# A two-layer hybrid backbone in f32 on one core: latent operands formed in place, early feed-forward products, chained transfers of the down projection

## The chip, the core and the metric

The kernel runs on one core of a Trainium2 chip. TensorE (PE) multiplies, VectorE (DVE) and GpSimd (POOL) work elementwise, ScalarE (ACT) applies functions of one operand, SyncE (SP) issues the DMAs. SBUF holds the operands, PSUM the products. The metric is the device time of one execution in microseconds; less is better.

## The reference

Two layers over 1024 latent and 256 context tokens of width 1024, all in f32. Layer 0 mixes by a convolution and a bidirectional state-space model, layer 1 by grouped-query attention, in which the context gives only keys and values. Each layer ends as follows (the context only in layer 0):

```python
x = layer_norm(ALPHA * x + g_m * y_lat, ln_g[l, 0], ln_b[l, 0])
x = layer_norm(ALPHA * x + g_f * swiglu(modulate(x, sh_f, sc_f), w_ffn_in[l], w_ffn_out[l]),
               ln_g[l, 1], ln_b[l, 1])
def swiglu(h, w_in, w_out):
    gate, up = jnp.split(h @ w_in, 2, axis=-1)
    return (jax.nn.silu(gate) * up) @ w_out
```

`y_lat` is the mixer's output behind its output projection; `g_m`, `sc_f`, `sh_f`, `g_f` are vectors made from the conditioning. The hidden width is 2816, 22 tiles of 128.

## The kernel before

Tokens lie along the free dimension, features along the partitions. The blocks `BLK` are 0 and 1 (512 latent tokens each) and 2 (256 context tokens, layer 0 only); a block's activations are eight tiles of 128 features, `acc(nb, k)`. Every f32 operand of a large product is split into two parts, a rounded `high` (L275, ScalarE) and the remainder `low` (L278, VectorE or GpSimd), and `mm3` (L293) makes three matmuls per product of tiles: high by high, high by low, low by high.

`out_proj` (L1597) runs blocks 0, 1 and, in layer 0, 2; for each of eight output tiles it loads and splits a weight (`weights`, L282 with L275 and L278), multiplies 24 times, loads the residual, scales it on GpSimd (L1626), adds the product on VectorE (L1627) and adds the tile to the running row sum on GpSimd (`add_up`, L411). Behind each block it starts `norm` (L444): a matmul with ones spreads the mean (L401), VectorE centres each tile (L449), ScalarE squares it (L452), VectorE adds the squares (L455), matmuls with a column of ones give the variance (L420), ScalarE takes the root (L423), VectorE the reciprocal (L424), matmuls broadcast the factor r over the partitions (L428), and ScalarE copies it to SBUF (L462). Then block 0 goes to `first_operands`, block 1 to `second_operands`, the context to `apply`. These multiply by r (L521, L531), form `a z + b` with gain a and bias b of the modulated norm on ScalarE (L541, L487) and VectorE (L543, L489), and split the result. The normalised tiles are stored to `res` by `put` for the residual of the down projection.

`ffn` handles gate and up, of both latent blocks, for one hidden tile f by seven products of 12 matmuls instead of eight (a Strassen-Winograd scheme). With A11, A12 the two feature halves of block 0 and A22 the second half of block 1, S1 to S4 are sums and differences of the halves of both blocks; on the weights' side B11, B12, B21, B22 and T1 to T4, made by `quads` (GpSimd's subtractions at L585, splits L275 and L278). The order in a tile is:

```python
p = multiply("A11", "B11")
p = multiply("A12", "B21")
late = multiply("S4", "B22")
seventh = multiply("S3", "T3")
p = multiply("S2", "T2")
p = multiply("S1", "T1")
p = multiply("A22", "T4")
```

In layer 0 the context's gate and up products (48 matmuls of 256 columns) follow in each tile; in tile 0 they stand behind S1 and need the context's norm. The hidden tiles, in two parts, go to DRAM (`hide`, L675).

The down projection (`run`) walks blocks 0, 2, 1 (layer 1: 0, 1), four output tiles at a time (`lower`, `upper`), over pairs j of hidden tiles. `last_weights` loads and splits the weights of a pair, `load` (L757) brings hidden tiles back from DRAM into 28 free slots, `residual` fetches `res` (L509) and scales it on GpSimd (L765 to L771).

Within a phase TensorE's order is pinned by `in_order`. VectorE, ScalarE, GpSimd and SyncE get their order from a scheduler that walks the program by estimated due times; each engine then works strictly in that order. `PACE` tables tell the scheduler how long a background task, such as a norm, takes between its steps. `fixed`, `hurry`, `loose` and `urgent` loosen or raise single instructions.

## Time and profile before

| | |
|---|---|
| Median of 3 runs | 2898.48 us (2891.24 to 2900.97) |
| Profiled execution | 2894.89 us, span from first to last instruction 2892.9 us |
| Mean granted clock of TensorE | 0.957 of full speed |
| Busy: TensorE, VectorE, GpSimd, ScalarE | 91%, 65%, 39%, 39% |
| DMA | 395.12 MB, mean 137 GB/s |
| TensorE waiting in `mm3` for an operand's high part | 50.0 us in 8 waits |
| TensorE waiting in `mm3` for a weight's high part | 27.2 us in 8 waits |

Names of tiles in the trace: `p` is a product in PSUM, `n` a mean, variance or r in PSUM, `hl`, `x`, `xr` hold operands, `wsplit` weights in two parts, `raw` weights as loaded, `acc` activations, `tmp` scratch, `hid` hidden tiles in DRAM, `res` stored activations in DRAM. A timeline row gives start, length, engine, line, operation, tiles written and read, the count of instructions run together and, in brackets, the engine's idle time before and what ended it. Some small f32 matmuls leave two records each.

### The profile page before, as it was taken

Reading aid. Unit: us, or ns where it says so; the run is one execution under the profiler, and the core shown is the slowest. Engines: PE = TensorE matmul, PEld = TensorE weight load, DVE = VectorE, ACT = ScalarE, POOL = GpSimd, SP = SyncE. Lnnn points to the kernel's source line nnn. Section 1 sums busy time; section 2 is a strip of 40 time slices with the busy share of each in tenths; the row PEclk is TensorE's granted clock in tenths of the full one; section 3 lists DMA queues with packets and bytes.
Section 4 is the critical chain, followed back from the end, with each engine's and each line's share of the span. In section 5 each row is a group of like instructions: output and inputs, shape, how many; then the busy total and the mean of one; then the engine's idle time right before and its main releaser. Section 6 shows DMA issues by size and latency. Waiting matters only on the chain.

```text
span 2892.9 us, 38248 instructions
## 1 busy us (share of the span) xinstructions
PE 2642.9 (91%) x14324; PEld 2223.6 (77%) x14324; DVE 1889.3 (65%) x2844; ACT 1119.3 (39%) x1943; POOL 1127.4 (39%) x994
## 2 busy tenths in 40 slices
PE   7867899949999999899999999999957999998998
PEld 4756777738888888788887778898846888886887
DVE  8876647887777655324458569998578666652244
ACT  5211216443333333123334348888344333331133
POOL 2799543444333433101035225554445444421111
PEclk9978999969999999999999999999978999999998
DMA  7322556314444222966444421112422323247634
GB/s 268 89 57 56 161 187 249 115 65 158 167 161 144 111 99 99 352 203 222 132 135 127 121 66 52 52 59 73 153 80 88 114 105 117 108 151 294 217 126 131
DMA packets 184233, 395.12 MB, mean 137 GB/s; under 512 B 38000, under 2 KB 74352, under 8 KB 177264
## 3 DMA queue, kind: packets, MB, share of 16 engines
q1 hardware_dynamic: 184048, 392.68, 40.3%
q8 instruction: 113, 1.85, 0.3%
q14 instruction: 72, 0.59, 0.1%
HBM read 305.11 MB, written 82.28 MB: 134 GB/s over the span
## 4 chain that ended last, share of the span: by engine, by line
PE 70%; DVE 10%; POOL 8%; DMA 7%; issue 2%; ACT 1%; SPq 1%; DVEq 0%; POOLq 0%; ACTq 0%
PE p L293 59%; PE q L293 3%; PE p L1874 3%; DMA raw<-w_ffn_out 2%; PE p L1857 2%; DVE const L1834 2%; DVE wsplit L278 1%; DVE tmp L531 1%; POOL acc L1020 1%; POOL acc L1023 1%; DVE const L1824 1%; DVE hl L278 1%; DMA hl<-hid 1%; DMA acc<-res 1%; PE p L1365 1%
## 5 line engine op out<-in xcount | busy, mean ns | idle before, releaser
L293 PE MATMUL p<-hl,wsplit 128*128 128x512 f32 (+1 forms) x5604 | 1201.2, 372 | 102.7 <-ACT hl L275 50.0
L293 PEld LDWEIGHTS p<-hl,wsplit 128*128 128x128 f32 x5604 | 973.9, 192 | 313.2 <-ACT hl L275 56.7
L278 DVE TENSOR_TENSOR wsplit<-raw,wsplit 128x1024 fp32r<-128x1024 f32 (+1 forms) x307 | 352.3, 1149 | 422.7 <-ACT wsplit L275 402.5
L275 ACT ACTIVATE wsplit<-raw 128x1024 fp32r<-128x1024 f32 (+1 forms) x368 | 316.0, 863 | 775.7 <-PE p L293 456.0
L293 PE MATMUL p<-x,wsplit 128*128 128x512 f32 (+1 forms) x1408 | 333.8, 384 | 1.3 <-DVE hl L1368 0.8
L293 PEld LDWEIGHTS p<-x,wsplit 128*128 128x128 f32 x1408 | 258.8, 190 | 53.4 <-ACT x L275 1.0
L667 DVE TENSOR_TENSOR tmp<-p,tmp 128x512 f32<-128x512 f32 x308 | 206.1, 684 | 67.9 <-PE p L293 59.2
L293 PE MATMUL p<-hl,acc 128*128 128x512 f32 x996 | 232.8, 389 | 0.0
L278 POOL TENSOR_TENSOR wsplit<-raw,wsplit 128x512 fp32r<-128x512 f32 (+1 forms) x61 | 101.8, 1672 | 315.3 <-ACT wsplit L275 308.9
L585 POOL TENSOR_TENSOR raw<-raw 128x512 f32<-128x512 f32 (+1 forms) x99 | 184.7, 1866 | 96.1 <-DVE wsplit L278 50.3
L293 PEld LDWEIGHTS p<-hl,acc 128*128 128x128 f32 x996 | 186.4, 188 | 38.3
L411 POOL TENSOR_TENSOR tmp<-tmp,acc 128x512 f32<-128x512 f32 (+1 forms) x54 | 85.6, 1586 | 251.6 <-DVE acc L810 184.3
L1874 PE MATMUL p<-hl,acc 128*128 128x256 f32 x960 | 150.8, 294 | 12.2 <-DVE hl L278 8.9
L1874 PEld LDWEIGHTS p<-hl,acc 128*128 128x128 f32 x960 | 130.3, 191 | 24.8 <-DVE hl L278 15.5
L278 POOL TENSOR_TENSOR hl<-tmp,hl 128x512 fp32r<-128x512 f32 (+1 forms) x56 | 84.4, 1524 | 111.5 <-ACT hl L275 46.7
L293 PE MATMUL q<-hl,wsplit 128*128 128x512 f32 (+1 forms) x576 | 125.2, 378 | 0.0
L1916 POOL TENSOR_TENSOR tmp<-tmp 128x1024 f32<-128x1024 f32 x32 | 77.1, 2410 | 118.9 <-DMA tmp<-w_mod_rows 80.5
L293 PEld LDWEIGHTS q<-hl,wsplit 128*128 128x128 f32 x576 | 102.0, 206 | 19.1 <-issue 3.9
L278 DVE TENSOR_TENSOR hl<-p,hl 128x512 fp32r<-128x512 f32 x160 | 106.4, 681 | 8.8 <-ACT hl L275 7.1
L275 ACT ACTIVATE hl<-p 128x512 fp32r<-128x512 f32 x160 | 95.5, 598 | 31.0 <-PE p L1857 29.5
L293 PE MATMUL q<-acc,raw 128*128 128x512 f32 x384 | 104.3, 407 | 0.3 <-ACT hl L1840 0.3
L585 POOL TENSOR_TENSOR acc<-acc 128x512 f32<-128x512 f32 (+1 forms) x33 | 62.1, 1882 | 97.6 <-DVE wsplit L278 56.7
(403 smaller groups left out, 4018.7 us busy)
## 6 DMA issues: line engine op xcount, KB each, us to landing
raw<-w_ffn_out SPq DMA_DIRECT2D x121, 512.0 KB, 3.7
raw<-w_ffn_in SPq DMA_DIRECT2D x33, 1024.0 KB, 4.9
hid<-acc SPq DMA_DIRECT2D x66, 512.0 KB, 2.6
hl<-hid SPq DMA_DIRECT2D x60, 512.0 KB, 7.2
acc<-w_mod_rows SPq DMA_DIRECT2D x32, 512.0 KB, 3.6
tmp<-w_mod_rows SPq DMA_DIRECT2D x32, 512.0 KB, 3.5
x<-w_mod SPq DMA_DIRECT2D x28, 512.0 KB, 8.5
raw<-w_out_ab SPq DMA_DIRECT2D x24, 512.0 KB, 3.7
```

The lines of the kernel that those rows point to most:

```text
L275: self.nc.scalar.activation(dst.bitcast(F32R), src, AF.Copy, scale=scale)
L278: (eng or self.nc.vector).tensor_tensor(dst.bitcast(F32R), src, high, op=ALU.subtract)
L293: self.nc.tensor.matmul(ps, a.bitcast(F32R), b.bitcast(F32R), start=start and i == 0, stop=stop and i == 2)
L411: eng.tensor_tensor(self.sums, self.total, x, op=ALU.add)
L531: tt = lambda out, x, y, op: nc.vector.tensor_tensor(out, x, y, op=op)
L585: nc.gpsimd.tensor_tensor(out, x, y, op=ALU.subtract)
L667: tt = lambda out, a, b: nc.vector.tensor_tensor(out, a, b, op=ALU.add)
L1020: v.tensor_tensor(t, ai, bi, op=ALU.mult)
L1834: v.scalar_tensor_tensor(m[:, 1:2], m[:, 0:1], work[i]["c"][:, u:u + 1], rq, op0=ALU.min, op1=ALU.mult)
L1857: nc.tensor.transpose(pt[:, o:o + 128], p, bd.pk("ident"))
L1874: nc.tensor.matmul(po, val.bitcast(F32R), part[:, j * 256:(j + 1) * 256].bitcast(F32R), start=kp == 0 and e == 0, stop=kp == 4 and e == 5)
L1916: nc.gpsimd.tensor_tensor(w, w, c_row, op=ALU.mult)
```

## The change

Four parts.

**Latent blocks.** `latents` takes the place of `norm` with `first_operands` or `second_operands`. It stores the centred tiles, not the normalised ones, to `res` while centring, and the factor r to a tensor `factor` of its own. The gain is multiplied in place together with r, read from PSUM; the differences that make S4, S2, S3 are taken of tiles without a bias, and the biases, which follow from C_BS and the gains, enter in the split (`parts`). All low parts are on VectorE. For block 1 the squares are summed by TensorE: 32 matmuls with a column of ones, four after each tile. Sums and differences overwrite the tiles of both blocks in place; `mixing` holds back S2 and what follows until the early products have been written down.

**Output projection.** Row sums go to VectorE, residual scaling to ScalarE, two tiles at a time. The last block takes the output tiles in the order 7, 6, 5, 4, 0 to 3 and uses the split weights of 4 to 7 that the block before left in `KEPT`.

**Feed-forward.** The products A11·B11 and A12·B21 of the first `AHEAD` tiles (1 in layer 0, 3 in layer 1) stand ahead of block 1's operands; S2 comes before S3; the splits of T2, T3 and T1 of tile 0 come early; the context's norm begins behind S3 of tile 0. In layer 1 GpSimd makes the low part of T4 instead of B21.

**Down projection.** Weights are fetched in a list of needs, three pairs ahead, and `queue` ties each weight, hidden-tile and residual transfer to the one before it in program order. Six hidden tiles are begun in the last feed-forward tile. `residual` loads the factor, multiplies it in on VectorE and scales on ScalarE.

```diff
+    def queue(self):
+        if self.queued is not None:
+            self.after(self.latest(), self.queued)
+        self.queued = self.latest()
...
+    def parts(self, dst, x, bias=None):
+        h, lo = dst
+        if bias is None:
+            self.high(h, x)
+            self.low(lo, x, h)
+        else:
+            self.nc.scalar.activation(h.bitcast(F32R), x, AF.Identity, bias=bias)
+            self.nc.vector.scalar_tensor_tensor(lo.bitcast(F32R), x, bias, h, op0=ALU.add, op1=ALU.subtract)
...
+    def latents(self, nb, i, total, res):
...
+        self.stat(mean, total)
...
+        def add_squares():
+            k, s = todo.pop(0)
+            for j in range(n // 128):
+                nc.tensor.matmul(pv[:, j:j + 1], s[:, j * 128:(j + 1) * 128], ones,
+                                 start=k == 0 and j == 0, stop=k == KT - 1 and j == n // 128 - 1)
+                self.loose()
...
+        for k in range(KT):
+            tt(z[k], z[k], mean, ALU.subtract)
+            s = self.g(squares.next(), n) if last else self.t(n) if k else sq
+            nc.scalar.activation(s, z[k], AF.Square)
+            if k % 2:
+                nc.sync.dma_start(res[k - 1:k + 1, :, off:off + n].rearrange("k p n -> p k n"),
+                                  self.g3(ACC + ACO[nb], KT, n)[:, k - 1:k + 1])
...
+        factor = self.g(squares.next(), n) if last else sq
+        nc.scalar.activation(factor, r, AF.Copy)
+        nc.sync.dma_start(self.factors[nb], factor)
+        gain = lambda k: nc.vector.scalar_tensor_tensor(z[k], z[k], self.gains(i, nb, k)[0], r, op0=ALU.mult, op1=ALU.mult)
+        bias = lambda k: self.gains(i, nb, k)[1]
+        if not last:
+            for k in range(KT):
+                gain(k)
+                self.parts(self.operand("A11" if k < 4 else "A12", k % 4), z[k], bias(k))
+                yield pace[4]
+            for k in range(4):
+                tt(z[k + 4], z[k], z[k + 4], ALU.add)
+            return
+        y = [self.acc(0, k) for k in range(KT)]
+        for k in range(4):
+            gain(k)
+            gain(k + 4)
+            tt(z[k], z[k], z[k + 4], ALU.add)
+            tt(y[k + 4], y[k + 4], z[k], ALU.subtract)
+            self.parts(self.operand("S4", k), y[k + 4])
+        while self.mixing:
+            yield 1.0
+        for k in range(4):
+            tt(y[k], z[k], y[k], ALU.subtract)
+            self.parts(self.operand("S2", k), y[k], bias(k + 4))
+        for k in range(4):
+            tt(y[k + 4], z[k + 4], y[k], ALU.subtract)
+            self.parts(self.operand("S3", k), y[k + 4])
+        for k in range(4):
+            self.parts(self.operand("S1", k), z[k], self.g(C_BS + k, 1))
+        for k in range(4):
+            self.parts(self.operand("A22", k), z[k + 4], bias(k + 4))
...
+        begun = [following[0]] + [early(f) for f in range(1, ahead)]
+        for f in range(ahead):
+            p = self.ps()
+            self.product(p, "A11", begun[f]["B11"])
+            nc.scalar.activation(gates[f][:, 512:], p, AF.Copy)
+            p = self.ps()
+            self.product(p, "A12", begun[f]["B21"])
+            tt(gates[f][:, :512], p, gates[f][:, 512:])
+        self.mixing = False
...
-        def last_weights(ds, j):
-            if (ds, j) not in ready:
-                ready[ds, j] = self.weights(ow[j:j + 2, :, ds[0] * 128:(ds[-1] + 1) * 128].rearrange("f p n -> p f n"))
-            return ready[ds, j]
+        def last_weights():
+            if wanted:
+                ds, j = wanted.pop(0)
+                ready.append(self.weights(ow[j:j + 2, :, ds[0] * 128:(ds[-1] + 1) * 128].rearrange("f p n -> p f n"), queue=True))
...
         def residual(nb):
+            if nb < 2:
+                r = self.g(self.sum_ring.next(), 512)
+                nc.sync.dma_start(r, self.factors[nb])
+                self.queue()
             for d in range(0, KT, 2):
                 self.fetch(res, nb, d)
+                self.queue()
                 for k in (d, d + 1):
...
-                    nc.gpsimd.tensor_scalar(a, a, self.g(o + 32 + k, 1), self.g(o + 40 + k, 1), op0=ALU.mult, op1=ALU.add)
+                    if nb < 2:
+                        nc.vector.tensor_tensor(a, a, r, op=ALU.mult)
+                    nc.scalar.activation(a, a, AF.Identity, scale=self.g(o + 32 + k, 1), bias=self.g(o + 40 + k, 1))
```

Three places show how the instructions move; the line numbers of the changed kernel differ (`mm3` is L308, `low` L291, an eviction L1771, `add_up` L429, the squares L565, the gain L604, a low part with a bias L542).

TensorE in layer 1, from the end of the output projection; `p_...` are products, `n_...` means, variances and r. Before:

```order
L293 MATMUL p_16192<-hl_141_3271,wsplit_68 128x512 x12
L293 MATMUL p_16206<-hl_141_3271,wsplit_68 128x512 x12
L401 MATMUL n_16059<-tmp_69,const_60 128x512
L420 MATMUL n_16084<-const_60,tmp_69 128x1 x4
L428 MATMUL n_16091<-const_60 128x128 x4
L293 MATMUL p_16221<-hl_142_3272,wsplit_68 128x512 x12
```

With the change:

```order
L308 MATMUL p_16080<-hl_141_3271,wsplit_68 128x512 x12
L308 MATMUL p_16094<-hl_141_3271,wsplit_68 128x512 x3
L419 MATMUL n_16098<-tmp_69,const_60 128x512
L308 MATMUL p_16094<-hl_141_3271,wsplit_68 128x512 x9
L308 MATMUL p_16116<-hl_141_3271,hl_509_15460 128x512 x3
L565 MATMUL n_16100<-const_60,tmp_69 128x1 x4
L308 MATMUL p_16116<-hl_141_3271,hl_509_15460 128x512 x6
L565 MATMUL n_16100<-const_60,tmp_69 128x1 x4
L308 MATMUL p_16116<-hl_141_3271,hl_509_15460 128x512 x3
L308 MATMUL p_16143<-hl_141_3271,hl_509_15460 128x512 x3
L565 MATMUL n_16100<-const_60,tmp_69 128x1 x4
```

A mean, a variance and a broadcast stood in a row behind two products; now the mean stands inside the second product, and the squares of single tiles stand between further products with the same `hl_141_3271` (A11, A12) and other weights.

VectorE in layer 1, from block 0's factor to block 1's centring (`acc_504...` is block 0, `acc_505...` block 1, `hl_141...` A11 and A12). Before:

```order
L521 TENSOR_TENSOR acc_504_15441<-acc_504_15441,tmp_69 128x512 x8
L489 TENSOR_SCALAR tmp_69<-acc_504_15441,const_60 128x512 x3
L1627 SCALAR_TENSOR_TENSOR acc_505_15442<-p_15907,const_60,acc_505_15442 128x512
L489 TENSOR_SCALAR tmp_69<-acc_504_15441,const_60 128x512 x2
L278 TENSOR_TENSOR wsplit_68<-raw_15420,wsplit_68 128x512
L489 TENSOR_SCALAR tmp_69<-acc_504_15441,const_60 128x512
L1627 SCALAR_TENSOR_TENSOR acc_505_15442<-p_15954,const_60,acc_505_15442 128x512
L489 TENSOR_SCALAR tmp_69<-acc_504_15441,const_60 128x512 x2
L1627 SCALAR_TENSOR_TENSOR acc_505_15442<-p_15999,const_60,acc_505_15442 128x512
L278 TENSOR_TENSOR wsplit_68<-raw_15420,wsplit_68 128x512 x3
L449 TENSOR_TENSOR acc_505_15442<-acc_505_15442,n_16059 128x512 x8
```

With the change (the eight gains, L604, stand just ahead):

```order
L542 SCALAR_TENSOR_TENSOR hl_141_3271<-acc_504_15455,const_60,hl_141_3271 128x512 x4
L429 TENSOR_TENSOR tmp_69<-tmp_69,acc_505_15456 128x512
L542 SCALAR_TENSOR_TENSOR hl_141_3271<-acc_504_15455,const_60,hl_141_3271 128x512
L1771 SCALAR_TENSOR_TENSOR acc_505_15456<-p_15957,const_60,acc_505_15456 128x512
L542 SCALAR_TENSOR_TENSOR hl_141_3271<-acc_504_15455,const_60,hl_141_3271 128x512 x3
L551 TENSOR_TENSOR acc_504_15455<-acc_504_15455 128x512
L1771 SCALAR_TENSOR_TENSOR acc_505_15456<-p_15999,const_60,acc_505_15456 128x512
L429 TENSOR_TENSOR tmp_69<-tmp_69,acc_505_15456 128x512
L551 TENSOR_TENSOR acc_504_15455<-acc_504_15455 128x512 x3
L291 TENSOR_TENSOR wsplit_68<-raw_15434,wsplit_68 128x512
L429 TENSOR_TENSOR tmp_69<-tmp_69,acc_505_15456 128x512
L551 TENSOR_TENSOR acc_505_15456<-acc_505_15456,n_16098 128x512 x8
```

The eight values with gain and bias (L489), whose low parts GpSimd made, have given way to eight low parts on VectorE (L542), pair sums of block 0 (L551) and row sums (L429).

SyncE in layer 1, around the start of the down projection. Before:

```order
L509 DMA acc_691_18978<-res_92 128x2x512
L757 DMA hl_142_3272<-hid_0_16027 128x1024
L757 DMA hl_142_3272<-hid_20_16047 128x1024
L282 DMA raw_15420<-w_ffn_out 128x2x512
L757 DMA hl_142_3272<-hid_1_16028 128x1024
L757 DMA hl_509_15446<-hid_4_16031 128x1024
L757 DMA hl_509_15446<-hid_2_16029 128x1024
L757 DMA hl_509_15446<-hid_5_16032 128x1024
L757 DMA hl_509_15446<-hid_3_16030 128x1024
L282 DMA raw_15420<-w_ffn_out 128x2x512
L675 DMA hid_21_16048<-acc_534_16182 128x1024 x2
L282 DMA raw_15420<-w_ffn_out 128x2x512
```

With the change:

```order
L295 DMA raw_15434<-w_ffn_out 128x2x512 x2
L807 DMA hl_141_3271<-hid_6_16036 128x1024
L807 DMA hl_141_3271<-hid_7_16037 128x1024
L295 DMA raw_15434<-w_ffn_out 128x2x512
L807 DMA hl_142_3272<-hid_8_16038 128x1024
L807 DMA hl_142_3272<-hid_9_16039 128x1024
L295 DMA raw_15434<-w_ffn_out 128x2x512
L807 DMA hl_142_3272<-hid_10_16040 128x1024
L807 DMA hl_142_3272<-hid_11_16041 128x1024
L784 DMA hid_21_16051<-acc_538_16292 128x1024 x2
L295 DMA raw_15434<-w_ffn_out 128x2x512
L807 DMA x_15458<-hid_12_16042 128x1024
```

Before, hidden tiles stood ahead of the weights of the second and third pairs; now a weight pair stands behind every second hidden tile, and the stores of the last hidden tile (`hid_21...`) stand ahead of the fifth pair.

## Rows read from the trace of the kernel before

**Rows 1.** The page: busy time of the engines, chain that ended last.

```profile
PE 2642.9 (91%) x14324; PEld 2223.6 (77%) x14324; DVE 1889.3 (65%) x2844; ACT 1119.3 (39%) x1943; POOL 1127.4 (39%) x994
...
PE 70%; DVE 10%; POOL 8%; DMA 7%; issue 2%; ACT 1%; SPq 1%; DVEq 0%; POOLq 0%; ACTq 0%
```

**Rows 2.** Stretches: length, engines' busy time (instructions), granted clock, DMA share, GB/s.

```profile
2240.00:2280.00 40.00, 40.00 (x178) 33.11 (x178) 27.08 (x36) 14.77 (x26) 17.58 (x11) 1.00 0.28 106
2040.00:2080.00 40.00, 40.00 (x178) 33.14 (x177) 13.98 (x14) 7.44 (x7) 21.63 (x15) 1.00 0.39 125
2149.40:2154.10 4.70, 3.92 (x16) 3.56 (x16) 0.61 (x2) 0.32 (x2) 0.00 (x0) 0.50 0.00 0
1203.38:1233.49 30.11, 21.90 (x72) 16.53 (x73) 6.12 (x5) 5.29 (x5) 8.31 (x10) 0.83 0.88 336
2619.64:2650.73 31.09, 18.96 (x72) 14.55 (x73) 4.90 (x4) 4.24 (x4) 6.82 (x8) 0.78 0.98 371
```

**Rows 3.** TensorE's timeline, layer 1: start, length, line, operation, count, [idle before].

```profile
2101.39 0.95 PE L420 MATMUL n<-const,tmp 128*128 128x1 f32 x8
...
2107.10 1.05 PE L428 MATMUL n<-const 128*128 128x128 f32 x8
2107.91 16.37 PE L293 MATMUL p<-hl,wsplit 128*128 128x512 f32 x71
...
2136.76 2.08 PE L401 MATMUL n<-tmp,const 128*128 128x512 f32 x2 [1.25 <-POOL tmp L411]
2149.52 1.84 PE L420 MATMUL n<-const,tmp 128*128 128x1 f32 x8 [10.69 <-DVE tmp L455]
2151.93 2.08 PE L428 MATMUL n<-const 128*128 128x128 f32 x8 [0.57 <-DVE const L424]
...
2200.60 5.60 PE L293 MATMUL p<-hl,acc 128*128 128x512 f32 x24
```

**Rows 4.** Waits of TensorE, 2060 to 2210: total, times, longest.

```profile
PE p L293 <- ACT hl L275: 25.4, 4, 10.0
```

**Rows 5.** VectorE's timeline, layer 1.

```profile
2089.26 1.21 DVE L278 TENSOR_TENSOR wsplit<-raw,wsplit 128x1024 fp32r<-128x1024 f32 x1
...
2105.72 2.36 DVE L278 TENSOR_TENSOR wsplit<-raw,wsplit 128x1024 fp32r<-128x1024 f32 x1 [0.16 <-ACT wsplit L275]
...
2124.89 0.74 DVE L1627 SCALAR_TENSOR_TENSOR acc<-p,const,acc 128x512 f32<-128x512 f32 x1
...
2154.67 4.90 DVE L531 TENSOR_TENSOR acc<-acc,tmp 128x512 f32<-128x512 f32 x8 [2.80 <-ACT tmp L462]
...
2165.24 0.68 DVE L278 TENSOR_TENSOR hl<-tmp,hl 128x512 fp32r<-128x512 f32 x1
```

**Rows 6.** TensorE's timeline, layer 0.

```profile
537.09 17.22 PE L293 MATMUL p<-hl,wsplit 128*128 128x512 f32 x87
...
559.18 3.13 PE L293 MATMUL p<-hl,wsplit 128*128 128x256 f32 x24 [0.53 <-DVE wsplit L278]
...
592.02 6.78 PE L293 MATMUL p<-hl,wsplit 128*128 128x512 f32 x24
...
654.88 7.79 PE L293 MATMUL p<-acc,wsplit 128*128 128x256 f32 x48 [9.06 <-ACT tmp L703]
```

**Rows 7.** VectorE's timeline, the context's norm in layer 0.

```profile
598.86 2.72 DVE L449 TENSOR_TENSOR acc<-acc,n 128x256 f32<-128x256 f32 x8
...
648.51 5.11 DVE L489 TENSOR_SCALAR tmp<-acc,const 128x256 f32<-128x256 f32 x8
```

**Rows 8.** TensorE's timeline, start of layer 1's down projection.

```profile
2631.21 8.40 PE L293 MATMUL p<-hl,wsplit 128*128 128x512 f32 x26 [11.57 <-ACT wsplit L275]
```

**Rows 9.** SyncE's timeline there (DMA issues).

```profile
2584.05 0.38 SPq L282 DMA_DIRECT2D raw<-w_ffn_out  x1
...
2619.69 0.38 SPq L282 DMA_DIRECT2D raw<-w_ffn_out  x1
```

**Rows 10.** TensorE's timeline, start of layer 0's down projection.

```profile
1208.70 9.04 PE L293 MATMUL p<-hl,wsplit 128*128 128x512 f32 x24 [5.32 <-ACT wsplit L275]
```

More of the change, by code (lines that the diff above doesn't have):

```diff
@@ L564, in quads @@
+    def quads(self, layer, f, direct, first=True):
         nc = self.nc
@@ L576, in split @@
             self.hurry()
-        split("B11", b11)
-        split("B21", b21)
+        if first:
+            split("B11", b11)
+            split("B21", b21)
         split("B22", b22)
@@ L732, in ffn @@
             if f == FT - 1:
-                last_weights(lower, 4)
+                last_weights()
             tt(gate2, p, gate2)
@@ L737, in ffn @@
             if f == 0:
-                following = self.quads(layer, 1, context)
+                following = self.quads(layer, 1, context, 1 >= ahead)
+            gate = gates[0]
         if after:
@@ L1610, in out_proj @@
             bd.finish(before[nb])
-        for d in range(KT):
-            if nb == blocks[1] and d == 1:
+        order = (7, 6, 5, 4, 0, 1, 2, 3) if nb == blocks[-1] else range(KT)
+        for step, d in enumerate(order):
+            if mods and nb == blocks[1] and step == 1:
                 bd.finish(*mods)
```

237 lines of the change are left out of this document (143 added, 94 removed).

## Prediction

> **What bounds the kernel now.** The shares of the page come first: TensorE is busy 91% of the span, VectorE 65%, and the chain that ended last is 70% TensorE, 10% VectorE, 8% GpSimd and 7% DMA [rows 1]. So time can only be won where TensorE stands still or runs slowly. The table of stretches says where that is not: in a feed-forward stretch TensorE is busy 40.00 of 40 us, 178 matmuls, 0.2247 us each [rows 2]. A product of 12 matmuls takes 2.7 us there, a group of 24 takes 5.4 us. VectorE (27.08), ScalarE (14.77) and GpSimd (17.58) have room.
>
> TensorE's timeline shows where it stands. In layer 1 the output projection's last group and tile 0's first product end at 2124.3 (2107.91 + 16.37), and tile 0's last product ends at 2203.3 (2200.60 and half of the 24 that follow) [rows 3]: 79 us for a tile whose remaining work is 16.2 us. The table of waits puts 25.4 us of it on four gaps before S4's operands [rows 4]; another 10.69 stands ahead of the variance [rows 3]. Layer 0 has the same gap between 592 and 655 [rows 6]. The third place is the start of the down projections: in layer 1 TensorE waits 11.57 us for a weight split [rows 8], and wait and 72 matmuls together take 31.09 us (2619.64 to 2650.73) instead of 16.2 [rows 2]: a loss of 14.9. SyncE had issued one weight load at 2584.05 and the next only at 2619.69, behind 28 other transfers [rows 9]. In layer 0 the wait is 5.32 [rows 10], and 72 matmuls from its start on take 30.11 [rows 2]: a loss of 13.9.
>
> **Layer 1, from the projection to tile 0.** In the change out_proj leads to latents, which forms the operands in place; its order on VectorE sets the new time, so I add it up with the durations of rows 5: 0.61 us for a two-tensor operation in a run (4.90 for 8), 0.68 alone, 0.74 for the eviction with a PSUM operand, which I also take for the gain (it reads r in PSUM). The bias form (a low part with a bias) is not in this trace: bounds 0.61 and 0.74, I take 0.68, since it reads SBUF alone.
> Block 0's r is broadcast 9 matmuls later in its group than before, so at 2108.2 + 2.0 = 2110.2 [rows 3]. VectorE then has, up to the last row sum, 8 gains (5.9), 3 evictions (2.2), 8 low parts (5.4), 4 pair sums (2.4), 3 row sums (1.8), one weight part (0.7): 18.4 us, to 2128.6. Before, the mean started at 2136.76, behind GpSimd [rows 3].
> From the mean to the last square TensorE's pinned order holds 54 product matmuls (12.1 us) and 32 squares; four squares are eight records of 0.95 us [rows 3], so 7.6 us. With 1.0 for the mean: 2149.3. Square root, reciprocal and broadcast took from 2151.36 (2149.52 + 1.84) to 2154.01 (2151.93 + 2.08) [rows 3]; 2.6 us give 2151.9. This chain is no shorter than the old one, but four products of tiles 1 and 2 lie in it (10.8 us that the tiles no longer need).
> After r VectorE has 8 gains (5.9), 12 two-tensor operations (7.3), 8 bias lows (5.4), 8 lows of S4 and S2 (5.2), 4 differences and 4 lows of S3 (5.2): 29.0, to 2180.9. Behind S3's last low come 3 matmuls, then S1 and A22: 6.1 us, to 2187.0, against 2203.3. The stretch wins 16.3 + 10.8 = 27.1.
> The clock takes some back. After TensorE had stood 10.69 us the eight variance records took 1.84 us against 0.95 elsewhere, the broadcast 2.08 against 1.05 [rows 3]: the granted clock was 0.50 there [rows 2], 1.2 instead of 2.4 GHz. The changed order leaves one wait of some 4 us before the mean. Layer 0's 24 product matmuls after waits took 6.78 instead of 5.4 [rows 6]; I take such a 1.4 once, with bounds 0 and 19.7 (everything from mean to r at half clock, the whole of 12.1 + 7.6 again). **Sum: 25.7, taken as 25 us**; bounds 8 (the clock's 19.7) and 33 (r as early as centring alone would let it be, 7 us of squares less).
>
> **Layer 0.** The context block follows block 1 and starts at 554.3 (537.09 + 17.22) [rows 6]. Its 8 groups at 3.13 [rows 6], the squares (7.6) and 1.5 for mean and broadcast make 34.2, to 588.5; the squares cost TensorE time here, where the old block had waits for weight splits (0.53 ahead of a group [rows 6]). r stands 37 small matmuls (4.8) before the end: 583.7. VectorE: 8 gains (5.9), the operand work as above with 3.0 of evictions and sums (15.7), S4 and S2 lows (5.2), S3 (5.2), early weight parts and evictions (2.7): to 618.4. The context norm now follows S3: centring 8 of 0.34 (2.72) [rows 7], squares' sums and three evictions 7, root and broadcast 4, scaling 2.7 and forming 5.1 [rows 7], the last low 1: to 641. The context's gate products start there, at 654.88 before [rows 6]; what stands behind them is the same. **14 us**; 5 if the context's norm waits for tile 0's other products as now (9 us), 22 if its centring finds VectorE free between S4's and S3's lows (8).
>
> **Down projections.** Weights and hidden tiles are now issued in the order of need, three weight pairs ahead: 1.5 MB for every step of 5.4 us, 280 GB/s, under the 371 GB/s that the old start moved [rows 2]. The stores of the last hidden tile still stand in SyncE's queue, ahead of the fifth weight pair; they wait for the last tile's VectorE work, some microseconds behind its last product, and that pair is needed 21 us later. The factor loads (0.25 MB a block) and the four residual loads are spread in between. **28 us of the 28.8 go**, 14 if only one of the two starts is mended.
>
> **What costs nothing.** Residual scaling goes from GpSimd to ScalarE: in layer 1, 16 operations at between 0.57 (14.77 / 26) and 1.06 us (7.44 / 7) each, 9 to 17 us, beside one weight split every 5.4 us on an engine busy 7.44 of 40 [rows 2]; if the residual's DMA came late the splits behind it in ScalarE's queue would wait, some 5 us. Row sums on VectorE: 8 of 0.61 per block beside the dense projection, VectorE busy 13.98 of 40 in block 0. The factor's 8 multiplications a block lie beside dense down products. Four fewer weight splits in the last block: only in cover, except in layer 0's context block, counted above.
>
> **Sum.** 25 + 14 + 28 = 67 us off the profiled execution of 2894.89 gives 2828; that execution lies 3.6 us (0.12%) under the median of the runs, so I predict 2830. The bounds give 27 (8 + 5 + 14) to 83 (33 + 22 + 28): 2812 to 2871 around the median. A measurement of this kernel can tell some 0.3%, 8.7 us.
>
> **Rivals.**
> *The queue is not mended.* The chained transfers stand behind one another: if the stores of hidden tile 21 or the residual loads hold SyncE, the wait for weights moves a few steps on instead of going. For it: the queue is in order, and a wait at its head stops the weights too. Against: three pairs are ahead. Time: 2830 + 28 = 2858; chance 0.13.
> *Half of the transitions.* ScalarE forms the eight high parts of A22 and S1 ahead of S4's and sits behind squares, copies and table loads; if it, not VectorE, sets each low, the 25 + 14 shrink to the early products' 10.8: 2830 + 28.2 = 2858 as well; chance 0.13.
> *VectorE slowed by GpSimd: slower than before.* In this trace one VectorE low of 128x1024 took 2.36 us at 2105.72, where GpSimd added, and 1.21 at 2089.26 [rows 5]. The changed transitions put some 47 us of VectorE work in layer 1 and 45 in layer 0 on the path. At double price throughout they would cost 92 more: 2830 + 92 = 2922. It decides from a mean price 73% higher (67 of 92) on. Against it: the order shows GpSimd almost empty there, its lows and sums gone. Chance 0.06.
> The Trainium skill ("SBUF — State Buffer", section "SBUF: two separate sides") says that a VectorE operation with two SBUF inputs and a GpSimd operation that reads SBUF exclude each other for a whole instruction; the 2.36 against 1.21 agrees, and by that rule an emptied GpSimd keeps VectorE at the lower price.
> *It changes nothing measurable.* The early products only change places with the tiles' own, and both partial cases together leave 10.8 of the 67; a mean in layer 1 halfway back to the old one (4 of 8 us [rows 3]) leaves 7, under what can be told: 2892; chance 0.05.
> The Trainium skill ("TensorE: Matmul & The Clock Gate", section "What's actually happening") calls the throttled clock the default that activity releases; by that rule the early products would keep the higher clock through the statistics and give back the 1.4 us, 2829.
>
> **How the numbers follow.** Forecast 0.63, the two partial cases 0.13 each, slower 0.06, no change 0.05. The likeliest is 2830. Leaving out the last two (0.11) and the tails of the others, the range runs from 2806 (all bounds good, and 6 us for the relief of engines that I priced at nothing) to 2872. Faster by over 0.3%: 0.63 + 0.26 = 0.89; within: 0.05; slower: 0.06.
>
> **What would show it.** Right: in layer 1 the mean 5 us behind the end of tile 0's first product instead of 12; A22 of tile 0 some 16 us earlier, and tiles 1 and 2 a product pair shorter; in layer 0 the context's gate some 14 us earlier, measured from the end of block 1's projection; no wait above 2 us at either down start, and a weight load every third transfer on SyncE. Wrong: a new wait in the tiles, where GpSimd now has T4's low part instead of B21's in layer 1; VectorE's lows at 1.2 us in the transitions; or granted clock still near 0.6 in them.

## The result and the profile after

The changed kernel takes 2824.36 us (median of 4 runs, 2822.47 to 2826.97), the kernel before 2894.86 beside it: a ratio of 0.9756, 95% interval 0.9732 to 0.978, or 70.5 us less. The forecast was 2830, faster. The profiled execution has a span of 2824.8 us, where the one of before has 2892.9 (68.1 less).

The page of the changed kernel, shares and chain [rows 1]:

```profile
PE 2644.6 (94%) x14436; PEld 2234.9 (79%) x14436; DVE 1859.5 (66%) x2899; ACT 1158.4 (41%) x2003; POOL 935.1 (33%) x839
...
PE 76%; DVE 9%; POOL 8%; DMA 4%; ACT 1%; issue 1%; SPq 1%; DVEq 0%; POOLq 0%; ACTq 0%
```

TensorE is busy for almost as long as before, in a span 68 us shorter, and DMA has fallen from 7% of the chain to 4. The next table cuts both traces at the same places of the program; each number is a difference of two starts on TensorE's timeline.

| stretch | before | after | change | forecast |
|---|---|---|---|---|
| layer 0: end of block 1's projection to the first product behind the context's gate | 108.2 | 96.1 | −12.1 | −14 |
| layer 0: the first 144 matmuls of the down projection | 46.6 | 32.6 | −14.0 | −13.9 |
| layer 1: start of tile 0's first product to its last operand A22 used | 81.7 | 65.8 | −15.9 | −16.3, clock +1.4 |
| layer 1: tiles 1 to 21 | 399.9 | 389.0 | −10.9 | −10.8 |
| layer 1: the first 144 matmuls of the down projection | 47.6 | 32.6 | −14.9 | −14.9 |
| all else | 2208.9 | 2208.7 | −0.2 | 0 |

TensorE's timeline of the changed kernel in layer 1 answers to [rows 3]:

```profile
2093.64 3.56 PE L308 MATMUL p<-hl,wsplit 128*128 128x512 f32 x15
2100.24 1.61 PE L419 MATMUL n<-tmp,const 128*128 128x512 f32 x2 [3.04 <-DVE tmp L429]
2100.87 4.15 PE L308 MATMUL p<-hl,wsplit 128*128 128x512 f32 x9
...
2105.54 0.95 PE L565 MATMUL n<-const,tmp 128*128 128x1 f32 x8
...
2123.07 1.09 PE L595 MATMUL n<-const 128*128 128x128 f32 x8
2136.28 0.79 PE L308 MATMUL p<-hl,wsplit 128*128 128x512 f32 x1 [12.11 <-ACT hl L288]
2143.73 4.97 PE L308 MATMUL p<-hl,wsplit 128*128 128x512 f32 x11 [6.66 <-DVE hl L291]
...
2156.74 5.60 PE L308 MATMUL p<-hl,acc 128*128 128x512 f32 x24
```

Read it from the top: the projection ends at 2093.64, the mean waits 3.04 us for VectorE's last row sum (before, it waited for GpSimd), then products and squares fill TensorE until r (L595) at 2123.07. Behind r it stands for 12.11 and 6.66 us, while VectorE makes the operands; then all the rest of the tile follows without a gap. VectorE's timeline shows the list that it stands behind (before: [rows 5]):

```profile
2125.20 5.35 DVE L604 SCALAR_TENSOR_TENSOR acc<-acc,const,n 128x512 f32<-128x512 f32 x8 [1.24 <-ACT tmp L602]
...
2139.27 1.28 DVE L551 TENSOR_TENSOR acc<-acc,acc 128x512 f32<-128x512 f32 x2
2140.47 0.74 DVE L542 SCALAR_TENSOR_TENSOR hl<-acc,const,hl 128x512 fp32r<-128x512 f32 x1
...
2151.67 1.28 DVE L291 TENSOR_TENSOR xr<-acc,x 128x512 fp32r<-128x512 f32 x2
```

The eight gains (L604) come first, S3's last low parts end at 2152.95, and no other work stands between. The first gain starts 1.04 us behind the end of r's broadcast; the wait is put down to ScalarE's copy of r (L602), which stands behind an activation and a table load. In layer 0 the same chain lies beside the context block (before: [rows 6]):

```profile
567.31 2.74 PE L565 MATMUL n<-const,tmp 128*128 128x1 f32 x24
...
571.06 4.70 PE L565 MATMUL n<-const,tmp 128*128 128x1 f32 x24
576.83 3.41 PE L565 MATMUL n<-const,tmp 128*128 128x1 f32 x16
...
584.73 1.27 PE L595 MATMUL n<-const 128*128 128x128 f32 x8
...
634.19 0.58 PE L308 MATMUL p<-acc,wsplit 128*128 128x256 f32 x1 [1.15 <-ACT acc L505]
637.10 5.19 PE L308 MATMUL p<-acc,wsplit 128*128 128x256 f32 x18 [2.33 <-POOL acc L291]
...
648.16 5.63 PE L308 MATMUL p<-hl,acc 128*128 128x512 f32 x24
```

The 64 squares take 10.85 us here, not the 7.6 of full clock, and the context's gate (48 matmuls, 634.19 to 648.16) takes 14.0 us where it took 7.6: it starts 18.5 us earlier, counted from the projection's end, and 6.3 of these are lost in it again, at a granted clock of 0.56. VectorE's last operand of S3 and GpSimd's first low part of the context there:

```profile
617.72 0.67 DVE L291 TENSOR_TENSOR xr<-acc,x 128x512 fp32r<-128x512 f32 x1
```
```profile
636.28 1.46 POOL L291 TENSOR_TENSOR acc<-tmp,acc 128x256 fp32r<-128x256 f32 x2 [49.09 <-DVE tmp L507]
```

The starts of the two down projections of the changed kernel, as stretches (those of before: [rows 2]); they have no wait at all:

```profile
1166.69:1204.77 38.08, 38.08 (x170) 31.53 (x168) 18.76 (x24) 15.06 (x18) 0.00 (x0) 1.00 0.99 356
2548.40:2581.06 32.66, 32.66 (x145) 27.03 (x144) 15.40 (x19) 11.51 (x15) 0.00 (x0) 1.00 0.96 352
```

And SyncE's timeline ahead of layer 1's, where [rows 9] had one weight load and then none for 35 us:

```profile
2564.06 0.38 SPq L295 DMA_DIRECT2D raw<-w_ffn_out  x1
...
2565.49 0.43 SPq L890 DMA_DIRECT2D tmp<-factor  x1
2566.66 4.34 SPq L527 DMA_DIRECT2D acc<-res  x4
2572.00 0.37 SPq L295 DMA_DIRECT2D raw<-w_ffn_out  x1
```

### The profile page after: what moved, and what is told of

Its sections match the earlier page's. It is cut to its first block, busy times and chain, and to the rows that moved or that the text cites. A ratio compares the mean times of both kernels' runs of the same rounds, so it can differ in the third digit from the quotient of the medians.

```text
span 2824.8 us, 38374 instructions
## 1 busy us (share of the span) xinstructions
PE 2644.6 (94%) x14436; PEld 2234.9 (79%) x14436; DVE 1859.5 (66%) x2899; ACT 1158.4 (41%) x2003; POOL 935.1 (33%) x839
## 4 chain that ended last, share of the span: by engine, by line
PE 76%; DVE 9%; POOL 8%; DMA 4%; ACT 1%; issue 1%; SPq 1%; DVEq 0%; POOLq 0%; ACTq 0%
PE p L308 64%; PE q L308 3%; PE p L2017 3%; PE p L2000 2%; DVE const L1977 2%; PE p L1494 1%; POOL acc L1149 1%; POOL acc L1152 1%; DMA raw<-w_ffn_out 1%; DVE const L1967 1%; PE p L350 1%; DVE wsplit L291 1%; DVE acc L551 1%; DVE hl L291 1%; POOL tmp L1150 1%
## 5 line engine op out<-in xcount | busy, mean ns | idle before, releaser
L308 PE MATMUL p<-hl,wsplit 128*128 128x512 f32 (+1 forms) x5004 | 1066.4, 371 | 49.2 <-DVE hl L291 18.5
L308 PEld LDWEIGHTS p<-hl,wsplit 128*128 128x128 f32 x5004 | 871.1, 191 | 234.2 <-DVE hl L291 25.3
L288 ACT ACTIVATE wsplit<-raw 128x1024 fp32r<-128x1024 f32 (+1 forms) x340 | 289.4, 853 | 655.1 <-PE p L308 328.8
L291 DVE TENSOR_TENSOR wsplit<-raw,wsplit 128x1024 fp32r<-128x1024 f32 (+1 forms) x280 | 305.1, 1091 | 379.6 <-ACT wsplit L288 366.0
L308 PE MATMUL p<-x,wsplit 128*128 128x512 f32 (+1 forms) x1422 | 328.7, 380 | 0.8 <-DVE hl L1497 0.8
L308 PEld LDWEIGHTS p<-x,wsplit 128*128 128x128 f32 x1422 | 256.7, 188 | 51.4 <-ACT x L288 1.0
L291 POOL TENSOR_TENSOR wsplit<-raw,wsplit 128x512 fp32r<-128x512 f32 (+1 forms) x60 | 99.8, 1668 | 510.6 <-ACT wsplit L288 504.7
L308 PE MATMUL p<-hl,acc 128*128 128x512 f32 x972 | 226.3, 389 | 0.0
L308 PEld LDWEIGHTS p<-hl,acc 128*128 128x128 f32 x972 | 182.3, 188 | 37.9 <-DVE acc L291 0.2
L661 POOL TENSOR_TENSOR raw<-raw 128x512 f32<-128x512 f32 (+1 forms) x99 | 182.2, 1840 | 83.4 <-DMA raw<-w_ffn_in 56.1
L308 PE MATMUL q<-hl,wsplit 128*128 128x512 f32 (+1 forms) x576 | 124.8, 377 | 0.0
L308 PEld LDWEIGHTS q<-hl,wsplit 128*128 128x128 f32 x576 | 101.3, 204 | 19.4 <-issue 3.9
L308 PE MATMUL p<-hl,x 128*128 128x512 f32 (+1 forms) x528 | 114.1, 363 | 0.0
L291 DVE TENSOR_TENSOR hl<-p,hl 128x512 fp32r<-128x512 f32 x160 | 106.4, 681 | 8.4 <-ACT hl L288 6.8
L288 ACT ACTIVATE hl<-p 128x512 fp32r<-128x512 f32 x160 | 95.5, 598 | 32.0 <-PE p L2000 30.6
L308 PE MATMUL q<-acc,raw 128*128 128x512 f32 x384 | 104.2, 406 | 0.3 <-ACT hl L1983 0.3
L308 PEld LDWEIGHTS p<-hl,x 128*128 128x128 f32 x528 | 91.1, 196 | 14.6 <-issue 1.0
L308 PE MATMUL p<-acc,wsplit 128*128 128x256 f32 x696 | 92.5, 291 | 3.9 <-POOL acc L291 2.7
```

Source lines behind the costliest of these rows:

```text
L288: self.nc.scalar.activation(dst.bitcast(F32R), src, AF.Copy, scale=scale)
L291: (eng or self.nc.vector).tensor_tensor(dst.bitcast(F32R), src, high, op=ALU.subtract)
L308: self.nc.tensor.matmul(ps, a.bitcast(F32R), b.bitcast(F32R), start=start and i == 0, stop=stop and i == 2)
L661: nc.gpsimd.tensor_tensor(out, x, y, op=ALU.subtract)
```

## The experiments

The sum came out; what it does not tell is which edit earns what, and whether r, VectorE's list or the clock sets the time that is left in the transitions. The theory under test: the order of transfers on SyncE earns the down projections' 28.8 us; the transitions earn the rest, and their chain runs from the mean over r to VectorE's last low part. The rivals: the prefetch rather than the order; GpSimd's relief; the early products; the squares on TensorE. No run takes back the forming in place, or the low parts on VectorE, by itself: what these two earn is read from the traces. All times beside one set of runs of the kernel before each (2899.15, 2895.23 and 2894.61).

**The down part alone,** put on the kernel before (`last_weights`, `load`, `queue` and their calls; no other part of the change):

```diff
+                ready.append(self.weights(ow[j:j + 2, ...], queue=True))
...
                 nc.sync.dma_start(self.g(o, 1024), ...)
+                self.queue()
```

> The kernel before with the down projection's part alone (list of needs, three weight pairs ahead, six hidden tiles begun in the last tile, transfers chained). Theory of the sum: both starts become dense, 72 matmuls in 16.3 us from the start of each, 13.9 + 14.9 = 28.8 us less than before, nothing elsewhere: 2895 - 29 = 2866 us. Rival, that the two transitions carried more of the win than they show: under 20 us less, with waits for weight splits left at a start.

Measured: 2868.41 us, ratio 0.9898 (0.9883 to 0.9913): 30.7 less. Both starts are dense:

```profile
1178.82 38.24 PE L301 MATMUL p<-hl,wsplit 128*128 128x512 f32 x168
...
2584.75 38.24 PE L301 MATMUL p<-hl,wsplit 128*128 128x512 f32 x168
```

**The change without the chaining**: the same prefetch and the same list of needs, with the order of the transfers left to the scheduler.

```diff
     def queue(self):
-        if self.queued is not None:
-            self.after(self.latest(), self.queued)
-        self.queued = self.latest()
+        return
```

> The changed kernel with the prefetch three pairs ahead and the early hidden loads, but without the chain, so that the scheduler orders SyncE. Theory that the order on SyncE is what ended the stalls: hidden tiles move ahead of the weights again (some 25 between the second and the fifth pair), a wait of 5 to 15 us returns at each start: 20 to 35 us slower than the changed kernel, 2845 to 2860. Rival, that fetching three pairs ahead is enough by itself: within 6 us of the changed kernel.

Measured: 2858.45 us, 0.9862 (0.9847 to 0.9878): 40.7 us less than the kernel before beside it, where the changed kernel has 70.5 less, so some 30 slower than that (34 between the two medians). The tie that is missing here is one of order alone: it is a dependency of class `NoSync` (`after`), which makes no transfer wait for another to land. The waits are back, on TensorE:

```profile
1198.90 8.25 PE L306 MATMUL p<-hl,wsplit 128*128 128x512 f32 x24 [7.07 <-ACT wsplit L286]
...
2607.34 8.86 PE L306 MATMUL p<-hl,wsplit 128*128 128x512 f32 x24 [10.66 <-ACT wsplit L286]
```

and SyncE shows why:

```profile
2567.89 0.38 SPq L293 DMA_DIRECT2D raw<-w_ffn_out  x1
2569.13 6.50 SPq L805 DMA_DIRECT2D x<-hid  x5
...
2579.24 7.99 SPq L805 DMA_DIRECT2D hl<-hid  x7
2588.15 2.92 SPq L525 DMA_DIRECT2D acc<-res  x3
...
2595.88 1.65 SPq L293 DMA_DIRECT2D raw<-w_ffn_out  x2
```

Hidden tiles whose places are free go ahead of weights that are needed sooner, for 28 us. The two down starts take 47.9 and 46.7 us, as in the kernel before (46.6 and 47.6); they account for 29 of the 33 us by which the span is longer. So the order earns this part, and the prefetch without it earns nothing.

**One tile ahead in layer 1** instead of three.

```diff
-AHEAD = (1, 3)
+AHEAD = (1, 1)
```

> The changed kernel with one early tile in layer 1 as in layer 0 instead of three. In its trace the squares of block 1 stand each behind 6 matmuls of tiles 1 and 2, so r comes 24 us behind the mean. Theory that the early products and the squares only change places: r comes 11 to 13 us earlier, S4's operands with it, and tiles 1 and 2 take their 10.8 us back: 2822 to 2826 us, no difference. Rival, as my sum had it, that they fill time that is idle anyway: 10.8 us slower, 2835.

Measured: 2828.78 us, 0.9764 (0.9746 to 0.9782), not told apart from the changed kernel; it lies above the theory's range and 6 us under the rival. The profile is of the fastest run (2823.51; the others 2827 to 2831). Without the four products the squares stand close together and r comes 15.1 us behind the mean instead of 22.8:

```profile
2093.42 1.10 PE L419 MATMUL n<-tmp,const 128*128 128x512 f32 x2 [1.66 <-DVE tmp L429]
...
2096.42 11.51 PE L565 MATMUL n<-const,tmp 128*128 128x1 f32 x64
2108.50 2.08 PE L595 MATMUL n<-const 128*128 128x128 f32 x8 [0.57 <-DVE const L591]
2122.38 0.79 PE L308 MATMUL p<-hl,wsplit 128*128 128x512 f32 x1 [11.81 <-ACT hl L288]
```

Tile 0's A22 is used up 7.8 us sooner after the projection (1.4 of it because the mean waits 1.66 and not 3.04), and the 10.8 us of the products come back in tiles 1 and 2: a net of 3. In these traces the early products buy far less than their own length, because they delay r.

**Row sums and residual scaling back on GpSimd.**

```diff
-                    nc.scalar.activation(x, x, AF.Copy if b is None else AF.Identity, scale=g, ...)
+                    nc.gpsimd.tensor_scalar(x, x, g, 0.0 if b is None else b, op0=ALU.mult, op1=ALU.add)
...
-            bd.add_up(a, step, nc.vector)
+            bd.add_up(a, step, nc.gpsimd)
```

> The changed kernel with row sums and residual scaling of the output projection on GpSimd again, the low parts staying on VectorE. Theory: GpSimd was late before because it made block 0's low parts as well; with sums alone (1.3 to 1.7 us each against 5.4 us a group) it keeps up, VectorE loses 0.6 us a sum, the mean comes within 2 us of where it is: 2820 to 2828. Rival, that the sums on GpSimd themselves delayed the mean, or that GpSimd's work stretches VectorE's operations to 1.2 us there: mean 5 to 8 us later, 2830 to 2840.

Measured: 2821.98 us, 0.974 (0.9725 to 0.9755): no difference. The mean in layer 1 waits 3.71 us for GpSimd instead of 3.04 for VectorE:

```profile
2094.44 1.86 PE L419 MATMUL n<-tmp,const 128*128 128x512 f32 x2 [3.71 <-POOL tmp L429]
```

So the sums by themselves did not make the mean late before the change. What is left as the cause are the eight low parts that stood between them on GpSimd; no run puts these back alone. The move of sums and scaling is worth nothing here, and costs nothing. Of the rival one part is seen: beside a GpSimd subtraction of 2.39 us (L661, from 2079.25 on) a low part on VectorE took 2.78 us instead of 0.74:

```profile
2079.41 2.78 DVE L542 SCALAR_TENSOR_TENSOR hl<-acc,const,hl 128x512 fp32r<-128x512 f32 x1
```

The mean, counted from the projection's end, still came only 0.7 us later (7.27 and 6.60).

**The context's products of layer 0 later**, behind A22·T4 of tile 0.

```diff
-            if context and f == 0:
-                gate_of_context(f, w)
-                up_of_context(f, w)
             hide(f, 0, gate1, up1)
             p = multiply("A22", "T4")
+            if context and f == 0:
+                gate_of_context(f, w)
+                up_of_context(f, w)
```

> Changed kernel, with the context tile's two products of layer 0 placed behind tile 0's last product of the first kind (A22 with T4) instead of ahead of it. Theory (TensorE waits for the context's operands while a product whose operands are ready stands behind it): the wait of 2.3 us ahead of the context's products goes, 2821 to 2823 us, at the edge of what can be told. Rival (what was waited for is needed by the next step all the same): no change, 2823 to 2826 us.

Measured: 2823.15 us, 0.9752 (0.9734 to 0.9769): no difference. The product in front is run earlier, but the gate's own stall of 2.33 on GpSimd's low part stays, and a second one of 0.72 stands behind it.

**Operands in the order of use**: S4, S2, S3, S1, A22, each low part right behind its high part, on ScalarE and VectorE.

```diff
+        make("S4", lambda k: y[k + 4], s4)
...
+        make("S2", lambda k: y[k], s2, lambda k: bias(k + 4))
+        make("S3", lambda k: y[k + 4], s3)
+        make("S1", lambda k: z[k], none, lambda k: self.g(C_BS + k, 1))
+        make("A22", lambda k: z[k + 4], none, lambda k: bias(k + 4))
```

> Changed kernel, with tile operands formed after r in the order S4, S2, S3, S1, A22 on VectorE and ScalarE alike, so that S4's low parts no longer stand behind S1's and A22's. Theory (S4's products wait for low parts that come in the wrong order): the wait ahead of S4 in layer 1 falls from 12.1 us by 3 to 6, but the end of VectorE's whole list stays, so that tile 0's end moves only by the work that TensorE gets meanwhile: 2 to 5 us in layer 1 and 0 to 3 in layer 0, 2816 to 2822 us. Rival (what counts is the end of VectorE's list, since TensorE can run all products behind the last operand only): no change, 2823 to 2826 us; if the last products bunch up behind S1 and A22, up to 2830 us.

Measured: 2833.07 us, 0.9787 (0.9769 to 0.9805), some 9 slower than the changed kernel. S4's products start 5.7 us behind the start of r's broadcast instead of 13.2, and then TensorE meets many small waits and a new one:

```profile
2126.77 0.79 PE L308 MATMUL p<-hl,wsplit 128*128 128x512 f32 x1 [4.61 <-ACT hl L288]
...
2155.91 1.22 PE L308 MATMUL p<-hl,acc 128*128 128x512 f32 x2 [3.72 <-ACT acc L288]
2157.71 7.64 PE L308 MATMUL p<-hl,acc 128*128 128x512 f32 x22 [0.58 <-POOL acc L291]
```

VectorE's operand list now ends 33.0 us behind the end of r's broadcast instead of 28.8, with four evictions of products that had started meanwhile in it; the weight parts of the next product (`acc`, L288) come behind it on ScalarE, and the 24 matmuls that took 5.60 take 9.28 (2155.91 to 2165.19). What counts is the end of the lists, as the rival said, not the first operand.

**Squares summed by VectorE** again in block 1. The edit also lengthens the pace of the steps behind the centring (0.8 and 0.8 to 5.0 and 2.0).

```diff
-            s = self.g(squares.next(), n) if last else self.t(n) if k else sq
+            s = sq if k == 0 else self.g(squares.next(), n) if last else self.t(n)
...
-                todo.append((k, s))
-                if k >= 2:
-                    add_squares()
+                tt(sq, sq, s, ALU.add)
```

> Changed kernel, with the squares of block 1 in both layers summed by VectorE again and the column sums made by one short product for each 128 columns as before, instead of 64 small matmuls a layer on TensorE. Theory (TensorE's squares stand in the chain to r and, in layer 0's context block, have nothing to hide): layer 1's r comes 6 to 8 us earlier behind the mean, layer 0's context block loses some 5 to 10 us before its gate products, and the kernel takes 2806 to 2816 us. Rival (VectorE's seven sums of 0.61 us and its later evictions delay r as much as the matmuls did): 2822 to 2827 us; and if VectorE's work behind it moves too, up to 2835 us.

Measured: 2822.87 us, 0.9751 (0.9735 to 0.9766): no difference in time. In the trace r comes 17.0 us behind the mean instead of 22.8, layer 1's transition is 5.9 us shorter and layer 0's 1.5:

```profile
2103.53 1.10 PE L419 MATMUL n<-tmp,const 128*128 128x512 f32 x2 [3.04 <-DVE tmp L429]
...
2120.55 1.16 PE L446 MATMUL n<-const 128*128 128x128 f32 x8 [0.57 <-DVE const L442]
```

but from the down projection of layer 0 to the end of layer 1's output projection it takes 929.8 us, where the changed kernel took 927.0 and 924.7 in its two profiles. What the squares cost on TensorE is real in its stretch; whether the other 3 to 5 us belong to the edit, is the question of the next runs.

**That edit and the context's together**, beside the changed kernel once more:

> The changed kernel itself, unedited, timed beside the next three so that they share its chip. All theories: 2822 to 2827 us as before; the difference between its two sets of runs is the scatter that a verdict on the next three has to exceed.

> Changed kernel with the two edits together that took something off their stages in the traces: squares summed by VectorE in block 1, and the context tile's products behind tile 0's last product of the first kind. Theory (the stages add up: 7.4 us by the first, 1.2 by the second): 2814 to 2818 us. Rival (the several microseconds by which the attention of layer 1 differs from trace to trace belong to the edit, not to chance): 2820 to 2824 us, no difference from the changed kernel.

Measured: the changed kernel 2822.74 us (2821.14 to 2827.55, ratio 0.974 to 0.9766), the two edits 2822.03 (0.9736 to 0.9762). The nine runs of the changed kernel lie in two groups, five at 2821.14 to 2822.74 and four at 2826.22 to 2827.55, and both its profiles are of the second; so a few microseconds between two profiles need not be an edit's. Here the rival fits: layer 1's attention takes 930.1 us again, and near 1520 us the broadcast of a norm waits 4.81 instead of 1.87 (3.89 in the run before). All three kernels with squares on VectorE (the next one too) show 929.8 to 930.3 for this stretch, the eight profiles of the others that share the changed kernel's down projection 921 to 927. So the edit seems to have moved something there too, far from both places that it was made for; why, stays open.

**r earlier, with products behind it**: the kernel before this one and a shorter pace.

```diff
-... (2.0, 0.65, 5.0, 2.0, 0.0))
+... (2.0, 0.3, 1.5, 0.8, 0.0))
```

> The kernel before this one, with block 1's pace shortened as well, so that the variance stands behind 24 early product matmuls after the mean's group instead of 48, and 18 of them come behind r. Theory (VectorE could give the squares' sum some 3 us earlier than TensorE's order asks for it; matmuls behind r fill a wait that nothing else fills): r 2 to 3 us earlier behind the mean than the 17.0 of the kernel with squares on VectorE, the wait ahead of S4 4 us shorter, 2811 to 2816 us. Rival (the clock: fewer dense matmuls ahead of the statistics leave TensorE at half clock, as in the run with squares placed closer): no gain, 2818 to 2830 us.

Measured: 2824.57 us, 0.9756 (0.9742 to 0.9769). r came 18.8 us behind the mean, later than the 17.0, not earlier:

```profile
2117.35 1.83 PE L438 MATMUL n<-const,tmp 128*128 128x1 f32 x8 [4.19 <-DVE tmp L551]
2119.05 2.91 PE L308 MATMUL p<-hl,hl 128*128 128x512 f32 x6
2121.75 1.91 PE L446 MATMUL n<-const 128*128 128x128 f32 x8
```

The theory falls at VectorE: its last sum of squares came no earlier, so the variance, moved ahead, waits 4.19 us for it, and behind the wait variance, products and r ran at half clock (1.83 and 1.91 where 0.95 and 1.05 is usual), as the rival had it; whether for the rival's reason or for the wait, this run does not separate.

**Squares closer together**, behind every third product matmul, with 15 of them behind r (timed before the three runs above; the expectation of the last one refers to it).

```diff
-... (2.0, 0.65, 0.8, 0.8, 0.0))
+... (2.0, 0.6, 0.8, 0.8, 0.0))
```

> Changed kernel, with one number of block 1's pace made smaller (0.65 to 0.6), so that a square is placed behind every third product matmul instead of every sixth, and r's broadcast ends before the last 15 product matmuls instead of after them. Theory (the chain that sets tile 0's end in layer 1 runs through r, and r waits only for the place of the squares in TensorE's order): r comes some 7 us earlier behind the mean (16 instead of 23), the wait ahead of S4's products in layer 1 falls from 12.1 to about 6 us, and the kernel takes 2817 to 2820 us. Rival (VectorE, not r, sets the end: it makes the squares' inputs or is behind with other work): r comes earlier by less than 2 us or the wait stays, 2823 to 2826 us.

Measured: 2833.35 us, 0.9774 (0.9743 to 0.9805), of which one run 2817.45 and three 2831.04 to 2835.99. So it was timed again:

> The kernel with the squares placed behind every third product matmul once more, because its four runs lay far apart (2817 once, 2831 to 2836 three times). Theory (the granted clock decides: when the stretch of products and squares runs at half clock from the mean on, the four squares of 128 columns take 1.7 us and not 0.95, and r comes some 15 us later than at full clock): the runs fall in two groups, 2816 to 2820 and 2830 to 2837, and a profile shows 1.7 in the second, 0.95 in the first. Rival (ordinary scatter): runs spread evenly between 2817 and 2836.

Measured: 2819.87 us, 0.9751 (0.9728 to 0.9773): 2816.09, 2818.19, 2819.87, 2822.36 and once 2836.39. The first profile was of a run of 2835.66, the second of one of 2816.09. The same instructions in the first:

```profile
2103.83 1.70 PE L565 MATMUL n<-const,tmp 128*128 128x1 f32 x8
...
2131.26 1.05 PE L595 MATMUL n<-const 128*128 128x128 f32 x8
```

and in the second:

```profile
2096.48 0.95 PE L565 MATMUL n<-const,tmp 128*128 128x1 f32 x8
...
2111.93 1.05 PE L595 MATMUL n<-const 128*128 128x128 f32 x8
```

The stretches from mean to r, first and second run, with the granted clock behind the five engines:

```profile
2100.70:2132.00 31.30, 31.28 (x115) 27.33 (x116) 6.43 (x11) 10.89 (x15) 0.00 (x0) 0.56 0.18 68
```
```profile
2092.00:2115.00 23.00, 22.37 (x126) 19.02 (x127) 8.12 (x14) 11.98 (x17) 0.00 (x0) 0.93 0.27 100
```

The wait ahead of the mean is 3.04 us in both. In the second run half clock is granted at the mean (its two matmuls take 2.05 us) and full clock is back before the first squares; in the first the mean still takes 1.10, the clock falls behind it and stays down up to r, with TensorE busy for 31.28 of 31.30 us. r comes 30.5 us behind the mean or 19.3. The theory on the clock holds for these two runs, with 11 us in this place (15 expected), and four of the five new times lie in its two groups (2822.36 does not). At full clock the theory on r holds as well: r 3.5 us earlier than the changed kernel's, the transition 3.5 us shorter, and the five runs at 2816 to 2822 have a median of 2818.19, against 2822.47 over the fastest five of the changed kernel and 2822.74 over all nine. But four runs of nine take 2831 to 2836. No version tried here beats the changed kernel by more than runs scatter.

## Why the prediction was right, point by point

*Down projections: exact.* 28 of 28.8 us were forecast and 28.9 came; alone on the kernel before they give 30.7. The rival that the queue is not mended fell; the run without chaining shows its price, some 30 us where the rival had 28. The transfers moved 356 and 352 GB/s there, not the 280 of the forecast and close to the 371 of the old start, and hid all the same.

*Layer 1: the path was right, and its sizes nearly cancelled.* The wait before the mean was 3.0 us (forecast some 4), and r's broadcast ended 30.5 us behind the projection (2093.64 to 2124.16; forecast 30.3, from 2121.6 to 2151.9). In it the mean and the nine products behind it took 4.62 us (2100.24 to 2104.86) where 3.0 were priced at full clock: at a granted clock of 0.59 this is the clock's share, 1.6 by the rows and 1.4 by forecast. The squares made up for most of it, with 0.81 us from start to start and not 0.95. VectorE's list from r to S3's last low part took 28.8 us (29.0), but as 27.75 of work behind a wait of 1.04 for the copy of r, which the sum did not have. The gain with r cost 0.67 us and not 0.74, the low part with a bias 0.66 to 0.74 (0.68 taken). The half of the transitions that the second rival set at risk held: behind that one wait ScalarE waits for VectorE's gains (0.59 us at each), not the reverse. Of 27.1 us without the clock's share and 25.7 with it, 26.8 came.

*Layer 0: 12.1 instead of 14, as the balance of larger errors.* Counted from the end of block 1's projection, r's broadcast ended at 33.9 us (forecast 29.4): the squares were priced at full clock (7.6 us) and took 10.85. VectorE's last low part of S3 ended at 66.3 (64.1). The context's gate started at 82.1 (86.7), with the context's first high part, where the forecast had it wait for the whole of its operands. It ended at 96.1 (94.3): "what stands behind them is the same" was wrong, since a wait of 2.33 us for GpSimd's low part and half-clock matmuls took 6.3 us back. That errors of 2 to 6 us came out within 2 is in part luck.

*Costs at nothing: held, and more than that.* Scaling on ScalarE and sums on VectorE hide, as said; on GpSimd they would have hidden too. The "mean 5 us instead of 12" came with the sums on either engine: 3.9 us on VectorE, 4.6 on GpSimd.

*VectorE slowed by GpSimd: did not happen.* GpSimd ran nothing for 65 us of layer 1's transition, and VectorE's operations stayed at 0.61 (4.87 for 8). Where GpSimd did run beside a low part, that one was slowed, in the run with the sums on GpSimd (2.78 against 0.74) as before the change (2.36 against 1.21 [rows 5]). That a busy GpSimd would have cost the 92 us of this rival was not tested.

*Early products.* The accounting held: tiles 1 to 21 became 10.9 us shorter. As a gain of the edit it misleads: with two tiles fewer ahead the time is the same within what can be told (2828.78, 3 us more by the traces), since r comes 7.7 us sooner.

*The clock.* By the rule of the Trainium skill ("TensorE: Matmul & The Clock Gate", section "What's actually happening") the products ahead of r should have kept full clock. The changed kernel agrees from the first squares on, with 0.59 behind the mean and 1.00 from 2105 to 2123:

```profile
2100.87:2104.86 3.99, 3.99 (x11) 2.84 (x10) 2.96 (x5) 1.77 (x3) 0.00 (x0) 0.59 0.19 71
2105.00:2123.00 18.00, 18.00 (x113) 15.83 (x111) 3.24 (x6) 8.52 (x13) 0.00 (x0) 1.00 0.27 99
```

With the squares twice as dense one profiled run agrees and one does not, 0.93 against 0.56; by their times five runs of nine go with the first. The sign of being wrong, a granted clock still near 0.6 in the transitions, did not come: it was 0.82 over layer 1's (0.60 before) and 0.75 over layer 0's (0.73).

*The range.* Its lower end is some 3.6 us too low: 83 us off the median of 2898.48 is 2815, not 2812, and so 2809, not 2806. Layer 1's lower bound is 7.4 by its own terms (27.1 less 19.7), not 8. Neither touches the forecast.

## What to carry to other kernels

A queue that is served in order has to be filled in the order of need: a prefetch deep enough does nothing while transfers that happen to be free to start stand ahead of the one that is waited for, and one tie of order between neighbours in the queue was worth some 30 us here. A chain over one statistic (mean, variance, r) is read link by link; work that fills it pays only if it does not itself stand ahead of the next link, and what set the time here was the end of the longest list, not the first operand. Before an engine is relieved of work because it is late, look at what stands between its late instructions: here the sums could have stayed.

## What was not expected of the hardware

A nearly unbroken run of products and squares did not always come back to full clock. Squares of 128x1 in groups of 24 or 16 took 0.114, 0.196 and 0.213 us each one behind the other in layer 0; 64 in one go took 11.51 us, with a granted clock of 0.60; eight between three matmuls of 512 columns ran at 0.56 over 31 us in one run of a kernel and at 0.93 in another; eight between six took 0.95 us in all five profiles that have them in this form, at 1.00 in the changed kernel. The two profiled executions of that one kernel lie 19.6 us apart (2835.66 and 2816.09), 11.2 of it between mean and r and some 5 in layer 1's attention. What decides it in a single run, no trace here tells.
